# A two-layer trunk: three pairs of gate/up chunks per FFN in seven block products, weight sums by adding DMAs, rows normed before the transposes

## The chip, the cores and the metric

The kernel runs on one core of one Trainium2 chip. The metric is the device time of one execution in microseconds, as the median of the runs. The engines are called as in the profile: PE is the TensorE (PEld its weight loads), DVE the VectorE, ACT the ScalarE, POOL the GpSimd, SP the SyncE, which issues DMAs.

## What is computed

A trunk of two layers on 256 tokens of 1024 numbers, in float32. Each layer is a feed-forward network (FFN) as half a step, a mixer, and a second FFN as half a step; each has a norm ahead and one behind. The FFN's inner width is 2816. The mixer (three kinds of attention, gated and merged) is not changed by the edit beyond names of buffers.

```
def rms_norm(x, gain):
    xf = x.astype(jnp.float32)
    y = xf * lax.rsqrt(jnp.mean(xf * xf, axis=-1, keepdims=True) + NORM_EPS)
    return (y * gain.astype(jnp.float32)).astype(x.dtype)

def swiglu(x, wg, wu, wd):
    return (jax.nn.silu(x @ wg) * (x @ wu)) @ wd
...
    for l in range(DEPTH):
...
        x = x + 0.5 * rms_norm(swiglu(rms_norm(x, g_ffn1_pre[l]), ffn1_wg[l], ffn1_wu[l], ffn1_wd[l]),
                               g_ffn1_post[l])
...
        x = x + rms_norm(mixed, g_mix_post[l])
        x = x + 0.5 * rms_norm(swiglu(rms_norm(x, g_ffn2_pre[l]), ffn2_wg[l], ffn2_wu[l], ffn2_wd[l]),
                               g_ffn2_post[l])
    return x
```

## The kernel before

**Tiles.** The tokens are two tiles of 128, t = 0 and 1. The residual stays in SBUF (`xs`). All weights are streamed from HBM as half-blocks of 128 x 2048 float32 (1 MB each): 33 for an FFN, 40 for a mixer, 212 in all. An FFN is cut in 11 chunks of 256; a chunk's gate and up weights lie side by side, so a gate/up product is 512 columns wide. A gate/up half-block holds four k (blocks of 128 of the 1024 inputs) by 512 columns; a down half-block two k by 1024.

**Float32 by three products.** A weight w is split in whi (a copy by the ScalarE, L88) and wlo = w - whi (VectorE, L89), each in two halves of 1024; the transposed inputs likewise (L198, L199). A product is then hi by hi, hi by lo and lo by hi, three matmuls of 512 columns (`mm3`, L245, L247, L250; L273 in the last down product of a sublayer). One half-block for one token tile is a step of 12 matmuls.

**Order.** Two generators, one for each token tile, go through the trunk; tile 1 is three half-blocks behind tile 0 (`LAG`), and each half-block's split serves both. `Stream` loads ahead through the SyncE's queue into 3 raw buffers and splits into 6 pairs of split buffers. Small chains (transposes of h, attention) run beside the products, a step in each tick. The framework schedules each engine's instructions from the order of the code.

**An FFN** (`ffn`): `prenorm` takes x times the gain (`gained`, L211), transposes it on the TensorE (L197), and makes the reciprocal norm r: Square on the ScalarE (L163), then two steps on POOL (L155, and the power, L157). r enters only behind the products: Silu with scale r (L303), and h = up * r * silu (L305). h is transposed and multiplied by the down weights into an accumulator of two PSUM banks. `postnorm` takes the sums of squares of the accumulator by halves, r by POOL, y (L232), adds it to x (L233), and writes the next sublayer's gained input.

**Names** in rows: f010 is layer 0, second FFN, tile 0; m01 the mixer of layer 0, tile 1; gu the gate/up bank, acc the accumulator, hp a transposed h. PSUM holds two banks for gate/up, four for two accumulators, two for transposes.

Of the kernel before, what the change touches and what calls it, by code (L numbers as in the profile page):

```python
# [8 lines left out]
F32 = mybir.dt.float32  # L9
# [7 lines left out]
P = 128  # L17
# [4 lines left out]
L = 2  # L22
# [15 lines left out]
W_BUFS = 6  # L38
RAW_BUFS = 3
LEAD = 6            # quarter-blocks of weights split ahead of the first lane  # L40
LAG = 3             # half-blocks the second lane of tokens is behind the first
RAMP = 4            # half-blocks in which the lag grows by one at the start
# [3 lines left out]
REST_HEADS, REST_GATE, REST_FFN, REST_FFN_END = 6, 3, 4, 1  # L46
# [8 lines left out]
class Stream:  # L55
    """One half-block of weights after another: loaded, and split into two float32r parts
    whose sum is the float32 weight exactly."""

    def __init__(self, nc, wall, raw, wp):
        self.nc, self.wall, self.raw, self.wp = nc, wall, raw, wp  # L60
        self.raws, self.ready = {}, {}
        self.n = self.loaded = 0

    def load(self, j):
        """Loads run ahead of the splits."""
        while self.loaded < min(j, L * LAYER_BLKS):
# [7 lines left out]
    def split(self, n=1):  # L74
        """The next n quarter-blocks."""
        nc = self.nc
        for _ in range(n):
            i, h = divmod(self.n, 2)
            if i == L * LAYER_BLKS:
                return  # L80
            self.load(i + 1)
            if h == 0:
                self.ready[i] = [self.wp.tile([P, BLK], F32R, tag="w" + c, name=f"w{c}{i}")
                                 for c in ("hi", "lo")]
            c = slice(h * HALF, (h + 1) * HALF)
            hi, lo = (a[:, c] for a in self.ready[i])
            w = self.raws[i][:, c]
            nc.scalar.activation(hi, w, AF.Copy)  # L88
            nc.vector.tensor_sub(lo, w, hi.bitcast(F32))  # L89
            self.n += 1  # L90
            if h:
                self.load(i + 1 + RAW_BUFS)

    def get(self, j):
        self.split(max(0, 2 * (j + 1) - self.n))
        return self.ready[j]
# [3 lines left out]
def trunk(ctx: ExitStack, tc, x, wall, gpre, gpost, lamv, dgain, cst, out):  # L100
# [5 lines left out]
    ps = ctx.enter_context(tc.tile_pool(name="ps", bufs=2, space=PSUM))  # L106

# [9 lines left out]
    # The tensor engine's clock rises under load only: products of zeros until the inputs are here.  # L117
# [50 lines left out]
    def tick():  # L168
        """One step of each chain that began before this half-block."""
# [9 lines left out]
    def start(task):  # L179
        """A chain of small steps beside the products: one step in each half-block."""  # L180
# [24 lines left out]
    xg = {}  # L205
# [7 lines left out]
    def prenorm(t, i, name):  # L213
        """The gained inputs, transposed, and the reciprocals of their norms."""
        src = xg.pop(t)
        r = rstd_of([sumsq(xs[t], D, name)], D, 1, 1.0, name + "r", "rpre")
        xT = pair(KD, name + "T", "xT", NT)
        for a in (0, 4):
            split_T(src, xT, a, 4, f"{name}p{a}")
        yield  # L220
        return xT, r

    def postnorm(t, acc, i, scale, name):
        """Adds the normed product to the residual, by halves."""
        y = sp.tile([P, D], F32, tag="t4", name=name + "y", bufs=4)
        r = rstd_of([sumsq(acc[:, c], D // 2, name + str(n)) for n, c in enumerate(HALVES)],
# [504 lines left out]
```

## Time and profile before

| | us |
|---|---|
| median of the runs (1301.24 to 1301.8) | 1301.6 |
| span of the profiled execution | 1299.8 |
| TensorE busy | 1281.0 |
| VectorE busy | 750.9 |
| ScalarE busy | 707.0 |
| POOL busy | 38.0 |
| an FFN within the trunk, from one last accumulator to the next (451.2 to 640.1) | 188.9 |
| a mixer (189.0 to 451.2) | 262.2 |

The span is the time between the first and the last recorded instruction of one profiled execution, which takes a little less than a run's time. Busy times are sums of instructions on an engine; engines run side by side, so they don't add up to the span. Matmuls are pipelined: a row gives 0.39 us for one, while the next starts 0.23 us after it, so the distance of starts is what one costs.

### The profile page before, as it was taken

The page shows a single profiled execution, that of the slowest core. Times are in us where ns is not written, and L with a number is a line of the kernel's source. Part 1 is how long each engine was busy: PE and PEld are TensorE (multiplying, and loading weights), DVE is VectorE, ACT ScalarE, POOL GpSimd, SP SyncE. Part 2 cuts the span into 40 slices and gives each one's busy share as a digit, 9 for nine tenths or more (in the row PEclk, how much of TensorE's full clock was granted, in tenths as well). Part 3 has the DMA queues.
Part 4 walks back from the last instruction along what each step waited for, and adds up shares of the span by engine and source line. Part 5 has one row for each costly group of instructions (what it writes and reads, how often), then busy time and mean ns, then how long its engine had stood idle before and what let it go on. Part 6 is the DMA issues. An engine that isn't in the chain of part 4 may idle for free.

```text
span 1299.8 us, 15509 instructions
## 1 busy us (share of the span) xinstructions
PE 1281.0 (99%) x6178; PEld 1040.9 (80%) x6178; DVE 750.9 (58%) x973; ACT 707.0 (54%) x1033; POOL 38.0 (3%) x82
## 2 busy tenths in 40 slices
PE   8999999999999999999999999999999999999997
PEld 5888887888877878888788888788888787788885
DVE  6645457656566675445565545666665666644552
ACT  5545446678575554444554444656976655544441
POOL 0000001000000010000000000100000000000000
PEclk9999999999999999999999999999999999999999
DMA  8845555444534555555555555554344444555530
GB/s 310 309 163 194 187 178 202 147 162 136 188 130 171 185 195 194 193 179 183 190 198 191 194 190 179 181 195 162 130 163 164 160 165 174 196 194 185 179 123 32
DMA packets 34056, 232.37 MB, mean 179 GB/s; under 512 B 3904, under 2 KB 4032, under 8 KB 6976
## 3 DMA queue, kind: packets, MB, share of 16 engines
q1 hardware_dynamic: 33264, 230.28, 50.2%
q8 instruction: 48, 0.79, 0.2%
q10 hardware_dynamic: 720, 1.11, 0.2%
q14 instruction: 24, 0.20, 0.0%
HBM read 230.33 MB, written 1.05 MB: 178 GB/s over the span
## 4 chain that ended last, share of the span: by engine, by line
PE 92%; DVE 3%; ACT 2%; issue 1%; POOL 1%; DMA 1%; SPq 0%; POOLq 0%; DVEq 0%; ACTq 0%
PE f000gu L247 2%; PE f000gu L250 2%; PE f000gu L245 2%; PE f001gu L245 1%; PE f011gu L245 1%; PE f101gu L245 1%; PE f111gu L245 1%; PE f111gu L250 1%; PE f101gu L250 1%; PE f011gu L250 1%; PE f001gu L250 1%; PE f011gu L247 1%; PE f001gu L247 1%; PE f101gu L247 1%; PE f111gu L247 1%; PE f010gu L245 1%
## 5 line engine op out<-in xcount | busy, mean ns | idle before, releaser
L89 DVE TENSOR_TENSOR wlo<-raw,whi 128x1024 fp32r<-128x1024 f32 x424 | 506.4, 1222 | 301.2 <-ACT whi L88 300.8
L88 ACT ACTIVATE whi<-raw 128x1024 fp32r<-128x1024 f32 x424 | 432.0, 1055 | 226.0 <-PE f011gu L250 27.0
L245 PE MATMUL f000gu<-whi,f000Th 128*128 128x512 f32 x88 | 35.3, 401 | 0.8 <-ACT f000Th L198 0.8
L245 PE MATMUL f001gu<-whi,f001Th 128*128 128x512 f32 x88 | 35.1, 399 | 0.2 <-ACT f001Th L198 0.2
L245 PE MATMUL f011gu<-whi,f011Th 128*128 128x512 f32 x88 | 35.3, 401 | 0.0
L247 PE MATMUL f000gu<-wlo,f000Th 128*128 128x512 f32 x88 | 35.0, 398 | 0.3 <-DVE wlo L89 0.3
L245 PE MATMUL f111gu<-whi,f111Th 128*128 128x512 f32 x88 | 35.3, 401 | 0.0
L245 PE MATMUL f101gu<-whi,f101Th 128*128 128x512 f32 x88 | 35.2, 400 | 0.0
L250 PE MATMUL f000gu<-whi,f000Tl 128*128 128x512 f32 x88 | 34.9, 397 | 0.0
L245 PE MATMUL f100gu<-whi,f100Th 128*128 128x512 f32 x88 | 34.5, 392 | 0.0
L245 PE MATMUL f010gu<-whi,f010Th 128*128 128x512 f32 x88 | 34.5, 392 | 0.0
L245 PE MATMUL f110gu<-whi,f110Th 128*128 128x512 f32 x88 | 34.4, 391 | 0.0
L250 PE MATMUL f100gu<-whi,f100Tl 128*128 128x512 f32 x88 | 34.4, 391 | 0.0
L250 PE MATMUL f111gu<-whi,f111Tl 128*128 128x512 f32 x88 | 34.4, 391 | 0.0
L250 PE MATMUL f011gu<-whi,f011Tl 128*128 128x512 f32 x88 | 34.4, 391 | 0.0
L250 PE MATMUL f101gu<-whi,f101Tl 128*128 128x512 f32 x88 | 34.4, 391 | 0.0
L250 PE MATMUL f001gu<-whi,f001Tl 128*128 128x512 f32 x88 | 34.4, 390 | 0.0
L247 PE MATMUL f010gu<-wlo,f010Th 128*128 128x512 f32 x88 | 34.3, 390 | 0.0
L247 PE MATMUL f110gu<-wlo,f110Th 128*128 128x512 f32 x88 | 34.3, 390 | 0.0
L247 PE MATMUL f100gu<-wlo,f100Th 128*128 128x512 f32 x88 | 34.3, 390 | 0.0
L247 PE MATMUL f011gu<-wlo,f011Th 128*128 128x512 f32 x88 | 34.3, 389 | 0.0
L250 PE MATMUL f110gu<-whi,f110Tl 128*128 128x512 f32 x88 | 34.3, 389 | 0.0
(1889 smaller groups left out, 3154.6 us busy)
## 6 DMA issues: line engine op xcount, KB each, us to landing
raw<-wall_dram SPq DMA_DIRECT2D x211, 1024.0 KB, 4.8
gpre<-gpre_dram SPq DMA_DIRECT2D x6, 512.0 KB, 6.2
gpost<-gpost_dram SPq DMA_DIRECT2D x6, 512.0 KB, 4.0
raw<-wall_dram SPq DMA_DIRECT2D x2, 512.0 KB, 7.9
out_dram<-x ACTq DMA_DIRECT2D x4, 256.0 KB, 2.0
x<-x_dram SPq DMA_DIRECT2D x2, 256.0 KB, 3.0
x<-x_dram SPq DMA_DIRECT2D x1, 512.0 KB, 9.1
cs<-cst_dram SPq DMA_DIRECT2D x1, 352.0 KB, 11.5
```

The costliest lines, as they stand in the source:

```text
L88: nc.scalar.activation(hi, w, AF.Copy)
L89: nc.vector.tensor_sub(lo, w, hi.bitcast(F32))
L245: nc.tensor.matmul(o[:, n:n + 512], xh[:, k, :], wh[:, kk, n:n + 512], start=first, stop=False)
L247: nc.tensor.matmul(o[:, n:n + 512], xh[:, k, :], wl[:, kk, n:n + 512], start=False, stop=False)
L250: nc.tensor.matmul(o[:, n:n + 512], xl[:, k, :], wh[:, kk, n:n + 512], start=False, stop=last)
```

## The change

**Seven block products.** In each FFN the chunks (1,2), (4,5) and (7,8) are taken as pairs. Two token tiles by two halves of k, times two halves of k by two chunks, is a product of 2 x 2 blocks; instead of eight block products it is made of seven, p1 to p7. The left sides are blocks of the transposed inputs or their row sums S1 to S4 (`sums`, VectorE L408 and L411, ScalarE L410; the transposes are also kept unsplit for them, L276). The right sides are B11, B21, B22 and the sums T1 = B11 + B12, T2 = T1 + B22, T3 = B12 + B22 and T4 = T2 + B21 of the stored half-blocks, each made in place in a raw buffer. Each of the seven is split like a half-block and used for one step. So a pair is split seven times where it was four. T2 and T4 are added by the VectorE (L134, two of 128 x 1024 each); T1 and T3 by a DMA that POOL issues and that adds HBM's block onto the raw buffer (L118): T1's when B11 is split, T3's right behind the load of B12. Products collect in three PSUM banks X, Y and Z; results are combined by one copy (L465) and five VectorE steps of 128 x 512 for each pair. The other chunks (0, 3, 6, 9, 10) stay plain products.

**Rows normed first.** FFN inputs are x * r * gain (`normed`, L296) before they are transposed, so Silu and h take no r. The mixers keep the old way.

**Order and buffers.** `program()` writes out a list of steps; weights come in the order of use. W_BUFS is 5 and RAW_BUFS 5; the two transposing banks became `tr` and `z`, the latter shared with Z. Norm steps, splits of transposes and combinations are scheduled early (`soon`). In the last eight blocks of a mixer tile 1 is four half-blocks behind.

```diff
-W_BUFS = 6
-RAW_BUFS = 3
...
+W_BUFS = 5
+RAW_BUFS = 5
...
+DMA_SUMS = ("T1", "T3")
...
+    def recipe(self, k):
+        if isinstance(k, int):
+            return [("split", k, c, (k,) if c else (), 2) for c in range(2)]
+        name, (b11, b12, b21, b22) = k
+        at, plus, free = {"B11": (b11, None, ()), "T1": (b11, b12, ()), "B21": (b21, None, ()),
+                          "T2": (b11, b22, ()), "B22": (b22, None, ()),
+                          "T3": (b12, b22, (b12, b22)), "T4": (b11, b21, (b11, b21))}[name]
+        ops = [("add", at, plus, c) for c in range(2)] if plus is not None and name not in DMA_SUMS else []
+        ops += [("split", at, c, free if c else (), 2) for c in range(2)]
+        after = {"B11": ("T1", b11, b12), "T1": ("T2", b11, b22), "T2": ("T4", b11, b21)}.get(name)
+        if after and after[0] in DMA_SUMS:
+            ops += [("dma", *after[1:])]
+        return ops
...
+        while self.loaded < len(self.blocks) and len(self.raws) < most:
+            i = self.blocks[self.loaded]
...
+            if i in self.thirds:
+                self.add_by_dma(i, self.thirds[i])
+    def add_by_dma(self, at, plus):
+        self.nc.gpsimd.dma_start(self.raws[at], self.wall[plus], accum_op=ALU.add)
...
+        if op[0] == "dma":
+            self.add_by_dma(*op[1:])
+        elif op[0] == "add":
+            c = slice(op[3] * HALF, (op[3] + 1) * HALF)
+            nc.vector.tensor_add(self.raws[op[1]][:, c], self.raws[op[1]][:, c], self.raws[op[2]][:, c])
...
+    tr_tags = itertools.cycle(("tr", "z"))
+    def tr_tile(shape, name, tag=None):
+        return ps.tile(shape, F32, tag=tag or next(tr_tags), name=name, bufs=1)
...
+    def normed(t, i):
+        with soon():
+            r = rstd_of([sumsq(xs[t], D, f"n{i}{t}")], D, 1, 1.0, f"n{i}{t}r", "rpre")
+            xg[t] = sp.tile([P, D], F32, tag="t4", name=f"xg{i}{t}", bufs=4)
+            for c in HALVES:
+                nc.vector.scalar_tensor_tensor(xg[t][:, c], xs[t][:, c], r, gain("pre", i)[:, c],
+                                               op0=ALU.mult, op1=ALU.mult)
...
-            nc.vector.scalar_tensor_tensor(y[:, c], acc[:, c], r, g[:, c], op0=ALU.mult, op1=ALU.mult)
-            nc.vector.tensor_add(xs[t][:, c], xs[t][:, c], y[:, c])
-            if i + 1 < 3 * L:
-                gained(t, i + 1, c)
-            else:
-                nc.scalar.dma_start(out[t * P:(t + 1) * P, c], xs[t][:, c])
+            with soon():
+                nc.vector.scalar_tensor_tensor(y[:, c], acc[:, c], r, g[:, c],
+                                               op0=ALU.mult, op1=ALU.mult)
+                nc.vector.tensor_add(xs[t][:, c], xs[t][:, c], y[:, c])
+                if i + 1 == 3 * L:
+                    nc.scalar.dma_start(out[t * P:(t + 1) * P, c], xs[t][:, c])
+                elif (i + 1) % 3 == 1:
+                    gained(t, i + 1, c)
+        if i + 1 < 3 * L and (i + 1) % 3 != 1:
+            normed(t, i + 1)
...
+        def sums(self):
+            (a11, a12), (a21, a22) = ([quads[t][:, k:k + 4] for k in (0, 4)] for t in range(2))
+            self.S = {}
+            for n, o, x, op, y in (("1", a22, a21, ALU.subtract, a22), ("2", a22, a22, ALU.subtract, a11),
+                                   ("3", a11, a11, ALU.subtract, a21), ("4", a12, a12, ALU.add, a22)):
+                nc.vector.tensor_tensor(o, x, y, op=op)
+                hi, lo = self.S[n] = pair(4, f"{self.nm}S{n}", "k2", 8)
+                nc.scalar.activation(hi, o, AF.Copy)
+                nc.vector.tensor_sub(lo, o, hi.bitcast(F32))
+            quads.clear()
...
+            if n in "14":
+                t = 0 if n == "1" else 1
+                return [b[:, 4 * t:4 * t + 4] for b in self.xT[t]]
+            if n == "2":
+                return [b[:, 4:] for b in self.xT[0]]
+            return self.S[{"5": "1", "6": "2", "7": "3", "3": "4"}[n]]
...
+        def up(self, t, c, hb, k):
...
+                self.o[t] = ps.tile([P, 512], F32, tag="gu", name=f"{self.nm}{t}gu{c}")
+            for _ in block(self.o[t], [b[:, 4 * hb:4 * hb + 4] for b in self.xT[t]], k, hb == 0, hb == 1):
...
+        def seven(self, n, c, k):
...
+            bank = {"1": "X", "2": "X", "5": "Z", "3": "Z"}.get(n, "Y")
...
+            if n in "156":
+                tag = "z" if bank == "Z" else "gu"
+                o[bank] = ps.tile([P, 512], F32, tag=tag, name=nm + bank, bufs=1 if bank == "Z" else 2)
+            for _ in block(o[bank], self.left(n), k, n in "156", True):
+                pass
+            o = o[bank]
...
+            q = self.c
+            with soon():
+                if n == "1":
+                    q["s1"] = tmp("s1", "mg")
+                    nc.scalar.activation(q["s1"], o, AF.Copy)
+                elif n == "5":
+                    q["s15"] = tmp("s15", "mg")
+                    nc.vector.tensor_sub(q["s15"], o, q["s1"])
+                elif n == "2":
+                    self.act(0, c, o, tmp("h11", "tok"))
+                elif n == "6":
+                    q["u2"] = tmp("u2", "mg")
+                    nc.vector.tensor_add(q["u2"], o, q["s1"])
+                elif n == "3":
+                    nc.vector.tensor_sub(q["u2"], o, q["u2"])
+                    self.act(0, c + 1, q["u2"], q["u2"])
+                elif n == "7":
+                    nc.vector.tensor_sub(q["s15"], q["s15"], o)
+                    self.act(1, c + 1, q["s15"], q["s15"])
+                elif n == "4":
+                    nc.vector.tensor_add(q["s1"], q["s1"], o)
+                    self.act(1, c, q["s1"], q["s1"])
...
+    for i in range(MIX_BLKS):
+        lag = LAG if i < MIX_BLKS - 8 else LAG + 1
+        order += [(i + lag - 0.5, 1, j + i), (i, 0, j + i)]
...
+    def seven(c, e, rest, last=()):
+        r = iter(rest)
+        def more():
+            return [x for x in [next(r, None)] if x]
+        out = [p(c, "1"), u(0, e, 0), u(0, e, 1), p(c, "5"), p(c, "2")] + more()
+        out += [u(1, e, 0), u(1, e, 1), p(c, "6")] + more() + [p(c, "3")] + more()
+        return out + [p(c, "7")] + more() + [*last[:1], p(c, "4"), *last[1:]]
```

In the order of the program the change is to be seen at three places. First, POOL at the end of layer 0's mixer, where the second FFN begins. m00or and m01or are the reciprocals for the mixer's results, f010r the one of the next FFN's inputs. Before:

```order
L155 TENSOR_SCALAR m00or<-m00o0s 128x1 [waits Activation_49]
L155 TENSOR_SCALAR m00or<-m00o1s,m00or 128x1 [waits Activation_49,Pool_49]
L157 TENSOR_TENSOR m00or<-m00or,nhalf 128x1 [waits Pool_49]
L155 TENSOR_SCALAR f010r<-f010s 128x1 [waits Activation_49]
L157 TENSOR_TENSOR f010r<-f010r,nhalf 128x1 [waits Pool_49]
L155 TENSOR_SCALAR m01or<-m01o0s 128x1 [waits Activation_49]
L155 TENSOR_SCALAR m01or<-m01o1s,m01or 128x1 [waits Activation_49,Pool_49]
L157 TENSOR_TENSOR m01or<-m01or,nhalf 128x1 [waits Pool_49]
```

After; n20r and n21r are the FFN's reciprocals (the FFN is called f2 now), and raw is a raw weight buffer:

```order
L221 TENSOR_SCALAR m00or<-m00o0s 128x1 [waits Activation_49]
L221 TENSOR_SCALAR m00or<-m00o1s,m00or 128x1 [waits Activation_49,Pool_49]
L223 TENSOR_TENSOR m00or<-m00or,nhalf 128x1 [waits Pool_49]
L118 DMA raw_3636<-wall_dram 128x2048 [waits DMAHW3_49,DMAHW4_49,DMAHW2_49,DMAHW5_49,DMAHW1_49,DMAHW6_49,DMAHW0_49,DMAHW7_49,DMASW4_49,DVE_49]
L221 TENSOR_SCALAR n20r<-n20s 128x1 [waits Activation_49]
L223 TENSOR_TENSOR n20r<-n20r,nhalf 128x1 [waits Pool_49]
L118 DMA raw_3490<-wall_dram 128x2048 [waits DMAHW0_49,DVE_49]
L221 TENSOR_SCALAR m01or<-m01o0s 128x1 [waits Activation_49]
L221 TENSOR_SCALAR m01or<-m01o1s,m01or 128x1 [waits Activation_49,Pool_49]
L223 TENSOR_TENSOR m01or<-m01or,nhalf 128x1 [waits Pool_49]
L221 TENSOR_SCALAR n21r<-n21s 128x1 [waits Activation_49]
L223 TENSOR_TENSOR n21r<-n21r,nhalf 128x1 [waits Pool_49]
```

Two DMAs now stand among the small steps: the one for a T3 ahead of n20r, the one for a T1 ahead of m01or; each waits for loads or splits.

Second, the VectorE at the same place, from the scaling of the mixer's result to the first split transposes. Before:

```order
L232 SCALAR_TENSOR_TENSOR m00oy<-m00acc,m00or,gpost_3628 128x512 [waits Activation_49,Pool_49]
L232 SCALAR_TENSOR_TENSOR m00oy<-m00acc,m00or,gpost_3628 128x512
L233 TENSOR_TENSOR x_73<-x_73,m00oy 128x512 [waits DVE_49] x2
L211 TENSOR_TENSOR xg_3632<-x_73,gpre_3633 128x512 [waits DVE_49]
L89 TENSOR_TENSOR wlo_3649<-raw_3526,whi_3648 128x1024 [waits DMAHW1_49,Activation_49]
L211 TENSOR_TENSOR xg_3632<-x_73,gpre_3633 128x512 [waits DVE_49]
L89 TENSOR_TENSOR wlo_3649<-raw_3526,whi_3648 128x1024 [waits Activation_49]
L199 TENSOR_TENSOR f010Tl<-f010p_3675,f010Th 128x512 [waits Activation_49]
L89 TENSOR_TENSOR wlo_3721<-raw_3563,whi_3720 128x1024 [waits DMAHW2_49]
```

After:

```order
L323 SCALAR_TENSOR_TENSOR m00oy<-m00acc,m00or,gpost_3626 128x512 [waits Activation_49,Pool_49]
L323 SCALAR_TENSOR_TENSOR m00oy<-m00acc,m00or,gpost_3626 128x512
L325 TENSOR_TENSOR x_73<-x_73,m00oy 128x512 [waits DVE_49]
L274 TENSOR_TENSOR m01gT1l<-m01gp_3646,m01gT1h 128x512 [waits Activation_49]
L325 TENSOR_TENSOR x_73<-x_73,m00oy 128x512 [waits DVE_49]
L144 TENSOR_TENSOR wlo_3660<-raw_3434,whi_3659 128x1024 [waits DMAHW7_49,Activation_49]
L144 TENSOR_TENSOR wlo_3660<-raw_3434,whi_3659 128x1024 [waits Activation_49]
L144 TENSOR_TENSOR wlo_3693<-raw_3490,whi_3692 128x1024 [waits DMAHW0_49,Activation_49]
L144 TENSOR_TENSOR wlo_3693<-raw_3490,whi_3692 128x1024 [waits Activation_49]
L296 SCALAR_TENSOR_TENSOR xg_3687<-x_73,n20r,gpre_3688 128x512 [waits DVE_49,Pool_49]
L296 SCALAR_TENSOR_TENSOR xg_3687<-x_73,n20r,gpre_3688 128x512 [waits DVE_49]
L144 TENSOR_TENSOR wlo_3723<-raw_3538,whi_3722 128x1024 [waits DMAHW1_49,Activation_49]
L274 TENSOR_TENSOR f20Tl<-f20p_3714,f20Th 128x512 [waits Activation_49]
```

The multiplication that makes xg no longer follows the addition to x; four splits (L144) stand between, and it waits for POOL.

Third, the VectorE between two pairs of the second FFN. Before, splits, products h (L305) and split transposes (L199):

```order
L89 TENSOR_TENSOR wlo_4115<-raw_4000,whi_4114 128x1024 [waits DMAHW5_49,Activation_49]
L199 TENSOR_TENSOR f011hT2l<-f011hp_4109,f011hT2h 128x256 [waits Activation_49]
L89 TENSOR_TENSOR wlo_4115<-raw_4000,whi_4114 128x1024 [waits Activation_49]
L199 TENSOR_TENSOR f010hT3l<-f010hp_4134,f010hT3h 128x256 [waits Activation_49]
L89 TENSOR_TENSOR wlo_4153<-raw_4038,whi_4152 128x1024 [waits DMAHW6_49,Activation_49]
L89 TENSOR_TENSOR wlo_4153<-raw_4038,whi_4152 128x1024 [waits Activation_49]
L305 SCALAR_TENSOR_TENSOR f011h_4187<-f011gu_4139,f011r,f011s_4185 128x256 [waits DVE_49,Activation_49]
L89 TENSOR_TENSOR wlo_4192<-raw_4077,whi_4191 128x1024 [waits DMAHW7_49,Activation_49]
```

After, from B11's split of the pair (7,8) (wlo_4505) to T1's (wlo_4585, from the same raw buffer):

```order
L144 TENSOR_TENSOR wlo_4505<-raw_4413,whi_4504 128x1024 [waits DMAHW3_49,Activation_49]
L426 TENSOR_TENSOR f2c4u_4405<-f2c4u_4405 128x256 [waits Activation_49]
L144 TENSOR_TENSOR wlo_4505<-raw_4413,whi_4504 128x1024
L478 TENSOR_TENSOR f2c4s_4301<-f2c4s_4301,f2c4Y 128x512 [waits PE_49]
L144 TENSOR_TENSOR wlo_4524<-raw_4415,whi_4523 128x1024 [waits DMAHW4_49,Activation_49]
L426 TENSOR_TENSOR f2c4s_4301<-f2c4s_4301 128x256 [waits Activation_49]
L274 TENSOR_TENSOR f20hT_4457<-f20hp_4495,f20hT_4457 128x256 [waits Activation_49]
L144 TENSOR_TENSOR wlo_4549<-raw_4440,whi_4548 128x1024 [waits DMAHW5_49,Activation_49]
L274 TENSOR_TENSOR f21hT_4503<-f21hp_4543,f21hT_4503 128x256 [waits Activation_49]
L481 TENSOR_TENSOR f2c4s_4249<-f2c4s_4249,f2c4Y 128x512 [waits PE_49]
L144 TENSOR_TENSOR wlo_4585<-raw_4413,whi_4584 128x1024 [waits DMASW2_49,Activation_49]
L426 TENSOR_TENSOR f2c4s_4249<-f2c4s_4249 128x256 [waits Activation_49]
```

Combinations (L478, L481) stand among the splits, and T1's split waits for the adding DMA (DMASW) as well as for the ScalarE.

## Rows read from the trace of the kernel before

**Rows 1.** Page, busy us of each engine (share of the span), instructions.
```profile
PE 1281.0 (99%) x6178; PEld 1040.9 (80%) x6178; DVE 750.9 (58%) x973; ACT 707.0 (54%) x1033; POOL 38.0 (3%) x82
```

**Rows 2.** Page, the chain that ended last, share of the span by engine.
```profile
PE 92%; DVE 3%; ACT 2%; issue 1%; POOL 1%; DMA 1%; SPq 0%; POOLq 0%; DVEq 0%; ACTq 0%
```

**Rows 3.** Windows: stretch, length, busy us (instructions), granted clock, DMA share, GB/s.
```profile
207.00:455.00 248.00, 247.57 (x1317) 200.81 (x1316) 153.56 (x216) 161.86 (x246) 4.57 (x9) 1.00 0.46 164
...
470.00:643.00 173.00, 172.17 (x782) 141.52 (x782) 90.83 (x109) 79.10 (x108) 1.11 (x2) 1.00 0.54 189
...
1283.00:1300.00 17.00, 8.01 (x36) 5.99 (x34) 6.04 (x10) 2.80 (x9) 2.00 (x6) 0.86 0.16 62
```

**Rows 4.** Waits of the TensorE: us in total, times, longest us.
```profile
PE f000p L197 <- DVE xg L211: 2.1, 1, 2.1
...
PE f111p L197 <- DVE xg L211: 0.8, 1, 0.8
```

**Rows 5.** Timeline, TensorE, twelve matmuls: start us, us, line, operation.
```profile
186.29 0.39 PE L245 MATMUL f001gu<-whi,f001Th 128*128 128x512 f32 x1
...
189.01 0.39 PE L273 MATMUL f000acc<-whi,f000hT10h 128*128 128x512 f32 x1
```

**Rows 6.** Page, the costliest groups: out<-in xcount | busy, mean ns | idle before.
```profile
L89 DVE TENSOR_TENSOR wlo<-raw,whi 128x1024 fp32r<-128x1024 f32 x424 | 506.4, 1222 | 301.2 <-ACT whi L88 300.8
L88 ACT ACTIVATE whi<-raw 128x1024 fp32r<-128x1024 f32 x424 | 432.0, 1055 | 226.0 <-PE f011gu L250 27.0
```

**Rows 7.** Timeline within an FFN, VectorE: two splits back to back; a split transpose.
```profile
64.83 0.42 DVE L199 TENSOR_TENSOR f001hT2l<-f001hp,f001hT2h 128x256 fp32r<-128x256 f32 x1
...
78.19 2.36 DVE L89 TENSOR_TENSOR wlo<-raw,whi 128x1024 fp32r<-128x1024 f32 x2 [0.47 <-ACT whi L88]
```

**Rows 8.** VectorE's instructions by line and shape: busy us, mean ns.
```profile
L305 DVE SCALAR_TENSOR_TENSOR f101h<-f101gu,f101r,f101s 128x256 f32<-128x256 f32 x11 | 5.3, 484 | 23.8 <-ACT f101s L303 23.8
...
L232 DVE SCALAR_TENSOR_TENSOR m01oy<-m01acc,m01or,gpost 128x512 f32<-128x512 f32 x2 | 1.5, 750 | 1.1 <-POOL m01or L157 1.1
...
L548 DVE TENSOR_TENSOR m01bs<-m01bs,m01by 128x512 f32<-128x512 f32 x2 | 1.4, 689 | 2.5 <-PE m01by L250 2.5
```

**Rows 9.** Page, DMA: a queue's packets, MB, share; an issue's count, KB, us to landing.
```profile
q1 hardware_dynamic: 33264, 230.28, 50.2%
...
raw<-wall_dram SPq DMA_DIRECT2D x211, 1024.0 KB, 4.8
```

**Rows 10.** Timeline where layer 0's mixer ends and its second FFN begins.
```profile
453.57 0.39 PE L273 MATMUL m00acc<-whi,m00gT1l 128*128 128x512 f32 x1
...
454.00 0.60 ACT L163 ACTIVATE m00o0j<-m00acc 128x512 f32<-128x512 f32 x1 [0.73 <-PE m00acc L273]
...
455.79 0.55 POOL L157 TENSOR_TENSOR m00or<-m00or,nhalf 128x1 f32<-128x1 f32 x1
...
456.37 1.41 DVE L232 SCALAR_TENSOR_TENSOR m00oy<-m00acc,m00or,gpost 128x512 f32<-128x512 f32 x2 [1.66 <-POOL m00or L157]
...
457.70 1.28 DVE L233 TENSOR_TENSOR x<-x,m00oy 128x512 f32<-128x512 f32 x2
...
459.08 1.06 ACT L163 ACTIVATE f010j<-x 128x1024 f32<-128x1024 f32 x1 [0.35 <-DVE x L233]
```

**Rows 11.** Timeline of the start, a power on POOL beside VectorE work.
```profile
13.02 1.28 DVE L211 TENSOR_TENSOR xg<-x,gpre 128x512 f32<-128x512 f32 x2
...
14.22 1.22 DVE L89 TENSOR_TENSOR wlo<-raw,whi 128x1024 fp32r<-128x1024 f32 x1
14.44 1.41 POOL L157 TENSOR_TENSOR f001r<-f001r,nhalf 128x1 f32<-128x1 f32 x1
```

**Rows 12.** Timeline of the start, tile 0's norm and its gained input.
```profile
5.87 0.54 POOL L157 TENSOR_TENSOR f000r<-f000r,nhalf 128x1 f32<-128x1 f32 x1
...
8.40 1.29 DVE L211 TENSOR_TENSOR xg<-x,gpre 128x512 f32<-128x512 f32 x2 [7.29 <-DMA gpre<-gpre_dram]
```

More of the change, by code (lines that the diff above doesn't have):

```diff
@@ new lines, in room, with step @@
+    def room(self, k):
+        i = self.items.index(k, max(0, len(self.ready) - 1))
+        return i < W_BUFS or self.last[self.items[i - W_BUFS]] < self.now
+    def step(self):
+        nc = self.nc
+        k, op = self.ops[self.done]
+        self.load()
+        if op[0] == "dma":
[3 more added lines that the diff above has]
+            nc.vector.tensor_add(self.raws[op[1]][:, c], self.raws[op[1]][:, c], self.raws[op[2]][:, c])
+        else:
+            _, at, n, free, of = op
+            if k not in self.ready:
+                self.ready[k] = [self.wp.tile([P, BLK], F32R, tag="w" + c, name=f"w{c}{len(self.ready)}")
@@ L94, in get, with ahead @@
-    def get(self, j):
-        self.split(max(0, 2 * (j + 1) - self.n))
-        return self.ready[j]
+            for f in free:
+                del self.raws[f]
+        self.done += 1
+        self.load()
+    def ahead(self, most):
+        while self.done < len(self.ops) and most > 0:
+            k = self.ops[self.done][0]
+            if self.first[k] > self.now + AHEAD or not self.room(k):
+                return
+            self.step()
+            most -= 1
+    def get(self, k):
+        while k not in self.ready or (self.done < len(self.ops) and self.ops[self.done][0] == k):
+            self.step()
+        return self.ready[k]
@@ L524, in mixer @@
         nm = f"m{l}{t}"
-        xT, r = yield from prenorm(t, 3 * l + 1, nm)
+        pre = prenorm(t, 3 * l + 1, nm)
+        xT, r = next(pre)
+        next(pre)
+        yield
+        next(pre)
+        yield
         rq = sp.tile([P, 2], F32, tag="rq", name=nm + "rq", bufs=2)
@@ L576, in mixer @@
             n = f"{nm}{mx}"
[L577 removed]
+            y = ys[mx] = pair(4, n + "y", "mT", 8)
             if mx == "a":
@@ L644, in trunk, with run @@
-    go(1, False)
+    now = {}
+    gains_of = {}
+    def run(step, k):
+        kind, n, t, *a = step
+        l, sub = divmod(n, 3)
+        if k is not None:
+            waiting[:] = side
+            w.ahead(4)
+        else:
+            waiting[:] = []
+        if n not in now:
+            j = l * LAYER_BLKS + (0, FFN_BLKS, FFN_BLKS + MIX_BLKS)[sub]
+            now[n] = [mixer(t, l, j) for t in range(NT)] if sub == 1 else FFN(n, j)
+        if sub == 1:
+            next(now[n][t], None)
+        else:
+            getattr(now[n], kind)(t, *a, *((k,) if k is not None else ()))
+        if k is not None:
+            w.now += 1
@@ new lines, in trunk, with program @@
+    with tc.manual_schedule(engines={nc.scalar.engine, nc.vector.engine}):
+        normed(0, 0)
+        for _ in range(2):
+            w.step()
+        for n, (step, k) in enumerate(plan[:START]):
+            run(step, k)
+            if n == 1:
+                normed(1, 0)
+    for n, (step, k) in enumerate(plan[START:]):
+        if n == CONSTANTS:
+            constants()
+        run(step, k)
+def program():
+    out = []
+    for n in range(3 * L):
+        l, sub = divmod(n, 3)
+        j = l * LAYER_BLKS + (0, FFN_BLKS, FFN_BLKS + MIX_BLKS)[sub]
+        steps = mixer_steps(n, j) if sub == 1 else ffn_steps(n, j)
+        if n:
+            i = max(i for i, (_, k) in enumerate(out) if k is not None)
+            out.insert(i + 1, steps.pop(1))
+            out.insert(i, steps.pop(0))
+        out += steps
+    return out
```

292 lines of the change are left out of this document (161 added, 131 removed).

## The prediction

> **What bounds the kernel now.** Read first how busy each engine is: the TensorE is busy in 99% of the span, the VectorE in 58% [rows 1]. Then the chain that ended last: 92% of it lies on the TensorE [rows 2]. Then the waits: the largest that the TensorE shows is 2.1 us at the start, the next of its kind 0.8 [rows 4]; all that the view lists come to some 10 us. The windows say the same stage by stage: 172.2 of 173 us in a feed-forward network (FFN), 247.6 of 248 in a mixer; the granted clock is 1.00 there, the upper level, 2.4 GHz [rows 3]. So time can only be won by fewer products, and lost where the TensorE begins to wait. A product of 512 columns starts every 0.2267 us: twelve from 186.29 to 189.01 [rows 5].
>
> The profiled execution has a span of 1299.8 us; the median of the runs is 1301.6, so 1.8 us lie around the span. I sum against 1299.8 and add 1.8.
>
> **A. Fewer products.** By the planned order the kernel issues 5088 products of 512 columns before and 4944 after. This is seven block products where there were eight, three products of each of four k: 12 fewer for each of 12 pairs of chunks, 144 in all. The transposes stay as many. 144 x 0.2267 = **-32.6 us**. All of it lies on the path as long as nothing else comes to bind; it is also the most that the change can win.
>
> **B. Rows normed before they are transposed.** Before, the transposes needed only x times its gain, and the reciprocal norm came in later, at the Silu. Now they need Square of x, two POOL steps and a multiplication first. This counts at three places, where an FFN follows another sublayer (mixer to FFN twice, FFN to FFN once). The chain, from the rows of the first mixer's end [rows 10]: last product of token tile 0 at 453.57, over at 454.0; squares and POOL until 456.34 (2.4 us); two scalings and two additions until 459.0 (2.7); Square of x and its accumulator 1.25; POOL's two steps between 0.7 and 1.4; the first half of the multiplication 0.7. That makes 8.4 to 8.8 us. Over it lie, by the order of after, 44 products and four transposes of tile 1, about 10.4 us, so the bare chain is covered. But on the VectorE the order of after has four weight splits between the additions and the multiplication, 4 x 1.14 = 4.6 us [rows 7], of which the Square and POOL hide some 2.2. With them tile 0's first half is ready at about 11 us, 0.5 late. For tile 1 the cover is 36 products and four transposes, 8.7 us, against a chain of 8.4 plus one transposed split and a weight split that share the VectorE: 0.5 to 2 us late. Then the four row sums S1 to S4 (eight VectorE steps of 0.69 [rows 8]) crowd the next splits. I take +3 us for each place, **+9 us** (0, all covered, to +18, twice as much).
>
> Two things sit on POOL there. Its small steps run longer beside VectorE instructions that read two tensors from SBUF: the power took 0.55 us at 455.79 and 1.41 beside the splits near 14.44 [rows 10, 11]. The Trainium skill states this as a rule (SBUF — State Buffer, section "Who interferes with whom"): a VectorE instruction with two SBUF inputs contends with a GpSimd instruction that reads SBUF; by it each of 2 x 3 norms would come about 0.9 us later, +5 us, and the total some 1288; the two rows agree with it in sign. And POOL now issues the adding DMAs in order: in the order of after, tile 0's pre-norm stands behind the DMA that makes a T3, which waits until that block's load has landed.
>
> **C. A VectorE that is busier in the pairs.** A steady pair of 17 half-block steps costs the TensorE 204 x 0.2267 = 46.2 us and some 1.6 for transposes, 48 us. In it the VectorE has 12 blocks of two splits at 1.14 (27.4) [rows 7], four additions of 1024 (4.6, like a split), five combinations of block products at 0.69 (3.4), six products h at 0.48 (2.9) and six split transposes at 0.42 (2.5) [rows 7, 8]: 40.8 of 48 us, 85%, where it was 90.8 of 173 [rows 3]. It still fits, but bunching leaves less room: a split may come late behind a combination. Three places are tight: p2 must wait until p1's result is copied out of the bank that both use (about 0.6 us, hidden in steady pairs by the steps between, not in the first pair), T2 must be added and split between T1's and its own use, and five weight buffers stand where six stood. I take 0.4 us for each pair, **+5 us** (0 to +10; a gain is excluded, since the TensorE waits for nothing there before). The ScalarE adds 72 copies of 1024 elements (76 us at 1055 ns [rows 6]) and smaller ones, to about 62%: no bound.
>
> Over the whole span the VectorE goes from 751 to about 961 us: 72 splits and 48 additions at 1.22, 92 steps of 512 at 0.69.
>
> **D. The adding DMAs.** T1 = B11 + B12 can start only when B11 is split, and must be there before p5. In the order of after that leaves the transfer 9 to 11.6 us until T1's own split could begin, and the TensorE stalls only past some 13. No row shows such a DMA. The nearest is the plain load of 1 MB, 4.8 us from issue to landing, on queues whose packets take half of the engines' time [rows 9]. One that reads two operands is bounded below by 4.8 and, taken as two plain reads, comes to 9.6; four times the plain load, 19.2, is my upper bound. I take 9.6, nearest to the row: **0 us**. T3 has more than a step's time to spare. In a sentence apart: the Trainium skill (DMA: Bandwidth & Descriptors, section "Measured (HBM→SBUF, 128 partitions, SWDGE, issued from GpSimd)") gives 6.15 us for a plain megabyte issued from GpSimd, which no run here shows; with twice that, 12.3 us, an estimate, the sum would stay as it is.
>
> **E. The rest.** Start: POOL ends the reciprocal norm at 6.4 us, before the gain is there at 8.4 [rows 12], so norming first costs nothing there. Mixers: five weight buffers for six leave four steps of lead where there were six, and two in the last eight blocks (lag 4); a step is 2.7 us and a split 2.3, so 0 to +3 in all; I take 0. The end (8.0 us of products in the last 17 us [rows 3]) is not touched.
>
> **Sum.** 1299.8 - 32.6 + 9 + 5 + 0 = 1281.2 us of span, and 1.8 around it: **1283 us**.
>
> **Rivals.**
> 1. All covered: B and C cost 0 to 6 together, since the chain of 8.4 us is under its cover of 10.4. 1269 to 1276 us. For it: the TensorE waits nearly nowhere now. Against: four splits in front of the multiplication.
> 2. Losses a little larger than summed (B at its upper end or C at 10): 1292 to 1299.
> 3. POOL's queue holds the norms: a T3 DMA waits for a load that was issued late, and the norm behind it comes 5 us later, 3 x 5 = 15: 1298. It decides when the load lands later than 6.4 us after tile 0's last product.
> 4. The VectorE becomes the bound in the pairs: at full durations (1.22 for 1.14) the 40.8 us of a pair are 43.0, and if waits in between add a sixth, the pair takes 50.2 for 48: +2.2 x 12 = 26, 1309, slower. It decides where waits and work on the VectorE pass 48 us in a pair, and the whole gain is gone at 49.6. For it: 85% of busy time with many short dependences; against: half of it can be done early.
> 5. The adding DMAs are late: at 19.2 us each T1 stalls p5 by about 6 us, 12 x 6 = 72: about 1355, slower. The place is the wait of T1's split for its DMA, on ScalarE and VectorE, with all later splits queued behind it. It breaks even where a pair's net gain, 18.6 / 12 = 1.6 us, is used up: at about 14.6 us for a DMA. For it: no row shows an adding DMA's speed. Against: 9.6 is well below.
> 6. The change doesn't do what it says, and the TensorE's products come slower (a cadence of 0.233 would undo the whole gain: 4944 x 0.0063 = 31 us). Against: left and right operands have the same form. It is within the slower cases' chance.
>
> **How the numbers follow.** Forecast (1276 to 1292) 0.50; all covered 0.17; larger losses 0.10; POOL's queue 0.06; the VectorE 0.06; DMAs late 0.10; other 0.01. The range reaches from 1269 to 1301, which holds the first four, 0.83, less a little at the edges. A difference of 0.2% (2.6 us, 1299.0 to 1304.2) is about what a measurement of this kernel can tell from no change. Faster takes the first three and two thirds of the fourth, 0.81; the same 0.04; slower 0.15.
>
> **What would show it.** Right: 4944 products at the same 0.2267; an FFN within the trunk about 7 us shorter (8.2 less for products, 1.2 more for its pairs); the VectorE at 75%; the waits of the TensorE at f2, f3 and f5's first transposes 1 to 3 us each; the adding DMAs landing within 11 us. Wrong: p5 waiting for T1's split in every pair (rival 5); waits for weight splits all over the pairs (rival 4); POOL idle before a pre-norm because of a DMA (rival 3); waits inside the mixers (E).

## The result, and the profile after

The changed kernel takes 1312.9 us (1309.6 to 1314.2 in four runs) where the kernel before takes 1301.65: a ratio of 1.0087, interval 1.0072 to 1.0101. The forecast was 1283 us, with a range of 1269 to 1301. It is slower, not faster, and 30 us away from the forecast.

The page of the profiled execution (span 1310.9 us), busy time of each engine and the chain that ended last:

```profile
PE 1260.9 (96%) x6034; PEld 1018.4 (78%) x6034; DVE 931.4 (71%) x1185; ACT 787.4 (60%) x1149; POOL 72.1 (6%) x106
...
PE 34%; DMA 6%; DVE 4%; ACT 2%; POOL 1%; issue 1%; POOLq 0%; DVEq 0%; ACTq 0%; SPq 0%
DMA raw<-wall_dram 6%; DVE wlo L144 2%; ACT whi L143 1%; PE f51gu L344 1%; PE f51gu L339 1%; PE f51gu L341 1%; PE f50acc L339 1%; PE f50acc L341 1%; PE f50acc L344 1%; DVE raw L134 1%; PE f51acc L344 0%; PE f51acc L341 0%; PE f51acc L339 0%; PE m11b L339 0%; PE m11a L339 0%
```

Against [rows 1] the TensorE has 144 instructions less, as planned, but stands still for 50 us of the span where it was 19. In the chain, DMA into the raw weight buffers now holds 6%, against 1% in all in [rows 2]. The waits of the TensorE say where (us in total, times, longest):

```profile
PE f5c4Z L339 <- ACT whi L143: 6.5, 1, 6.5
PE f2c4Z L339 <- ACT whi L143: 3.6, 1, 3.6
PE f3c4Z L339 <- ACT whi L143: 3.4, 1, 3.4
PE f31hp L271 <- DVE f3c4s L426: 2.4, 1, 2.4
PE f00gu L339 <- DVE f0c4s L481: 2.4, 1, 2.4
```

f2c4Z is p5 of the pair (4,5) in the FFN f2: it waits for the split of T1. What [rows 9] was for plain loads, with the queue of POOL's DMAs (q0) new, on the page (a queue's packets, MB, share of 16 engines; then an issue's count, KB, median us to landing):

```profile
q1 hardware_dynamic: 33264, 230.28, 47.4%
q0 software_dynamic: 3456, 25.17, 10.0%
...
raw<-wall_dram SPq DMA_DIRECT2D x211, 1024.0 KB, 4.9
raw<-wall_dram POOLq DMA_DIRECT2D x24, 1024.0 KB, 11.4
```

An adding DMA lands after 8.1 to 18.0 us, 11.4 in the median. The stages, from the last product into tile 0's accumulator to the next (before; after; and two kernels of the experiments, all sums on the VectorE, and p5 moved):

| us | before | after | all sums on VectorE | p5 two steps later |
|---|---|---|---|---|
| to the end of the first FFN | 191.5 | 194.9 | 183.9 | 185.4 |
| first mixer | 262.1 | 261.1 | 261.1 | 261.1 |
| second FFN | 188.9 | 190.0 | 183.1 | 182.5 |
| third FFN | 188.6 | 190.3 | 181.9 | 181.3 |
| second mixer | 262.1 | 261.5 | 261.1 | 261.2 |
| fourth FFN | 188.8 | 193.5 | 182.8 | 183.8 |
| rest | 17.9 | 19.6 | 19.6 | 19.9 |

Each FFN should have become 8.2 us shorter (36 products of 0.2267), less what the new steps cost; instead each became 1.1 to 4.7 longer. The mixers are as they were.

One such wait in the timeline of after (start, us, engine, line, operation, and the idle time before):

```profile
520.50 1.83 POOL L118 DMA_DIRECT2D raw<-wall_dram  x2 [41.59 <-DVE wlo L144]
...
524.65 0.42 ACT L425 ACTIVATE f2c1s<-f2c1s 128x256 f32<-128x256 f32 x1 [0.23 <-DVE f2c1s L481]
...
534.82 0.39 PE L344 MATMUL f20gu<-whi,f20Tl 128*128 128x512 f32 x1
537.70 2.00 ACT L143 ACTIVATE whi<-raw 128x1024 fp32r<-128x1024 f32 x2 [12.63 <-DMA raw<-wall_dram]
538.78 2.36 DVE L144 TENSOR_TENSOR wlo<-raw,whi 128x1024 fp32r<-128x1024 f32 x2 [12.37 <-ACT whi L143]
...
538.80 0.79 PE L339 MATMUL f2c4Z<-whi,f2S1h 128*128 128x512 f32 x1 [3.60 <-ACT whi L143]
...
541.08 0.63 PE L339 MATMUL f2c4Z<-whi,f2S1h 128*128 128x512 f32 x1
...
541.51 0.63 PE L341 MATMUL f2c4Z<-wlo,f2S1h 128*128 128x512 f32 x1
```

At 520.50, when B11 is split, POOL issues two adding DMAs of the pair (4,5) together, T3's and behind it T1's. The first lands 8.6 us after its issue, the second, T1's, 16.4. (T3's goes first in six of the twelve pairs, the three (4,5) among them; in the first FFN and in the pairs (7,8) T1's does.) ScalarE stands for 12.6 us before T1's copy, with all that is queued behind it, and VectorE with it; the TensorE runs dry for 3.6 us. Then its products start 0.43 us apart (541.08, 541.51) instead of 0.227, at the lower of its two clock levels (1.2 GHz); the granted clock of the windows falls with it (stretch, length, busy us (instructions), granted clock, DMA share, GB/s):

```profile
520.00:540.00 20.00, 16.00 (x71) 12.40 (x69) 7.63 (x11) 4.57 (x8) 1.83 (x2) 0.94 0.91 253
540.00:560.00 20.00, 19.94 (x81) 16.25 (x82) 20.00 (x24) 14.03 (x20) 0.00 (x0) 0.89 0.36 129
```

Here this costs 2.0 us on top (ten starts, from 540.06 to 544.38, take 4.3 us instead of 2.3).

### The profile page after: what moved, and what is told of

Read it like the earlier page. It is cut to its first block, busy times and chain, and to the rows that moved or that the text cites. A ratio compares the mean times of both kernels' runs of the same rounds, so it can differ in the third digit from the quotient of the medians.

```text
span 1310.9 us, 15665 instructions
## 1 busy us (share of the span) xinstructions
PE 1260.9 (96%) x6034; PEld 1018.4 (78%) x6034; DVE 931.4 (71%) x1185; ACT 787.4 (60%) x1149; POOL 72.1 (6%) x106
## 3 DMA queue, kind: packets, MB, share of 16 engines
q1 hardware_dynamic: 33264, 230.28, 47.4%
q0 software_dynamic: 3456, 25.17, 10.0%
HBM read 255.49 MB, written 1.05 MB: 196 GB/s over the span
## 5 line engine op out<-in xcount | busy, mean ns | idle before, releaser
L144 DVE TENSOR_TENSOR wlo<-raw,whi 128x1024 fp32r<-128x1024 f32 x496 | 589.4, 1220 | 174.7 <-ACT whi L143 174.2
L143 ACT ACTIVATE whi<-raw 128x1024 fp32r<-128x1024 f32 x496 | 503.5, 1055 | 242.8 <-DMA raw<-wall_dram 94.3
L134 DVE TENSOR_TENSOR raw<-raw,raw 128x1024 f32<-128x1024 f32 x48 | 57.8, 1218 | 0.0
L118 POOL DMA_DIRECT2D raw<-wall_dram x24 | 21.7, 942 | 467.8 <-DMA raw<-wall_dram 216.7
L339 PE MATMUL f00gu<-whi,f00Th 128*128 128x512 f32 x40 | 17.4, 435 | 4.3 <-DVE f0c4s L481 2.4
L721 ACT ACT_TABLE_LOAD x12 | 15.4, 1283 | 6.4 <-PE m01bg L344 2.2
L341 PE MATMUL f00gu<-wlo,f00Th 128*128 128x512 f32 x40 | 16.7, 417 | 0.4 <-DVE wlo L144 0.4
L344 PE MATMUL f00gu<-whi,f00Tl 128*128 128x512 f32 x40 | 16.8, 419 | 0.2 <-DVE f00Tl L274 0.2
L339 PE MATMUL f30gu<-whi,f30Th 128*128 128x512 f32 x40 | 16.2, 404 | 0.1
L339 PE MATMUL f20gu<-whi,f20Th 128*128 128x512 f32 x40 | 16.2, 406 | 0.0
L339 PE MATMUL f50gu<-whi,f50Th 128*128 128x512 f32 x40 | 16.2, 405 | 0.0
## 6 DMA issues: line engine op xcount, KB each, us to landing
raw<-wall_dram POOLq DMA_DIRECT2D x24, 1024.0 KB, 11.4
```

Source lines behind the costliest of these rows:

```text
L118: self.nc.gpsimd.dma_start(self.raws[at], self.wall[plus], accum_op=ALU.add)
L134: nc.vector.tensor_add(self.raws[op[1]][:, c], self.raws[op[1]][:, c], self.raws[op[2]][:, c])
L339: nc.tensor.matmul(o[:, n:n + 512], xh[:, k, :], wh[:, kk, n:n + 512], start=first, stop=False, **kw)
L341: nc.tensor.matmul(o[:, n:n + 512], xh[:, k, :], wl[:, kk, n:n + 512], start=False, stop=False, **kw)
L344: nc.tensor.matmul(o[:, n:n + 512], xl[:, k, :], wh[:, kk, n:n + 512], start=False, stop=last, **kw)
L721: nc.scalar.activation(s, o, AF.Sigmoid, scale=r)
```

## Experiments

Theory A: what costs is an adding DMA that stands in front of a split which the in-order engines then wait for; T1's is late because another goes ahead of it or runs beside it, and because its split comes early in the order. Theory B: the VectorE is the bound in the pairs. Theory C: the bytes moved cost, by slower loads, wherever the DMAs stand. In the first expectations theory A is narrower: there T1's DMA is late only because it is second in its queue; runs 3 and 5 made it wider. Times are medians; all ratios are to the kernel before, run on the same chip (1299.7 to 1300.4 us).

**1. T3's DMA behind T1's split, in the code.**

```diff
             ops += [("dma", *after[1:])]
+        if name == "T1" and "T3" in DMA_SUMS:
+            ops += [("dma", b12, b22)]
...
-            if i in self.thirds:
-                self.add_by_dma(i, self.thirds[i])
```

> The one edit: T3's adding DMA is issued behind T1's split instead of right behind the load of its block, so T1's adding DMA no longer stands second. Theory A (T1's transfer is late because T3's goes ahead of it: 8 to 10 us alone, 14 to 18 as the second of two): the three waits of p5 in the pair (4,5), 3.4 to 6.5 us, go, and with them the slow products behind them; the FFNs lose about 6 to 10 us each, the time comes to 1285 to 1292. Theory B (the VectorE is the bound in the pairs, and T1's transfer only starts late because B11's split is late): at most 3 us less, 1309 to 1313. Theory C (adding DMAs and loads share engines, whichever goes first): about half, near 1300.

1312.67 us, 1.0113 (1.0065 to 1.0161; one of the four runs took 1325.1). It tells nothing of the theories: the scheduler put POOL's instructions in the same order as before, since T3's DMA depends on nothing that T1's split makes.

**2. No adding DMA, T1 and T3 split as they are.**

```diff
-        self.nc.gpsimd.dma_start(self.raws[at], self.wall[plus], accum_op=ALU.add)
+        pass
```

> No adding DMA at all: T1 and T3 are split as they stand, without the addition, so part of the computation is left out; all other instructions stay. This gives what the transfers cost in all. Theory A and C: 1280 to 1288, no wait of p5 for a split, loads back at about 5 us. Theory B: within 4 us of the changed kernel, 1309 to 1313, with the waits of h's transposes for the VectorE still there.

1275.81 us, 0.9808 (0.9791 to 0.9825): all that the adding DMAs cost is 37 us, more than any theory said. Theory B is out as the main cause.

**3. T1 alone by DMA**, T3 by the VectorE: `DMA_SUMS = ("T1",)`.

> T3 is added by the VectorE (24 more additions of 1024, 29 us in all), T1 still by DMA, alone in POOL's queue. Theory A: T1 lands within 8 to 11 us, p5's waits go, and 2.4 us more VectorE work for a pair costs 0 to 1 us each: 1285 to 1300. Theory B: slower than the changed kernel, 1315 to 1340.

1294.57 us, 0.9945 (0.9926 to 0.9964). T1's DMAs land in 8.1 to 11.3 us, and yet they cost 18.5 us against the run that follows. The timeline at the same pair shows how:

```profile
511.57 0.94 POOL L118 DMA_DIRECT2D raw<-wall_dram  x1 [40.23 <-DMA raw<-wall_dram]
...
516.93 0.69 DVE L481 TENSOR_TENSOR f2c1s<-f2c1s,f2c1Y 128x512 f32<-128x512 f32 x1
...
521.96 2.00 ACT L143 ACTIVATE whi<-raw 128x1024 fp32r<-128x1024 f32 x2 [5.10 <-DMA raw<-wall_dram]
...
523.87 0.40 ACT L425 ACTIVATE f2c1s<-f2c1s 128x256 f32<-128x256 f32 x1
...
524.88 0.66 PE L271 MATMUL f21hp<-ident,f2c1s 128*128 128x128 f32 x2 [2.94 <-DVE f2c1s L426]
...
526.62 0.63 PE L339 MATMUL f20gu<-whi,f20Th 128*128 128x512 f32 x1
...
527.05 0.63 PE L341 MATMUL f20gu<-wlo,f20Th 128*128 128x512 f32 x1
```

The Silu of the last pair's result (L425) had its input at 517.6, when L481 was done. It stands behind T1's copy on the ScalarE, which waits 5.1 us for the DMA; so the transposes of that h wait 2.9 us, and the products behind them start 0.43 us apart again. p5 itself does not wait in this FFN. What the TensorE wants first is not T1, but what stands behind T1 in a queue.

**4. All sums on the VectorE:** `DMA_SUMS = ()`.

> All four sums on the VectorE (48 more additions, 58 us). Theory A: no transfers to wait for; the VectorE's 40.8 us in a pair of 48 become 45.6, so it is close to the bound: 1290 to 1310. Theory B: 4.9 us more in each of 12 pairs, 1350 to 1370.

1276.04 us, 0.9811 (0.9794 to 0.9827): 58 us more of additions on the VectorE than in the changed kernel (53 more of its busy time), and 37 us less time. No expectation held. The page:

```profile
PE 1250.0 (98%) x6034; PEld 1015.2 (80%) x6034; DVE 984.6 (77%) x1233; ACT 788.6 (62%) x1149; POOL 52.1 (4%) x82
```

The VectorE has room even at 77%; against run 2, which leaves those additions out, they cost nothing that can be measured.

**5. T1's DMA really ahead of T3's:** as 1, with both kept in the order of the code on POOL.

> Both adding DMAs stay, but T1's now really goes ahead of T3's in POOL's queue (in the run before the scheduler had put T3's first again); T3's is issued right behind it. Theory A (what costs is that T1's transfer is second in its queue): T1 lands in 8 to 11 us and the time comes to that of the kernel with T1's DMA alone, 1291 to 1298. Theory C (each adding DMA costs by what it takes from the loads and from the other, in whichever order): 1307 to 1314, T1 landing in 11 us or more.

1305.25 us, 1.0034 (1.0014 to 1.0053), between the theories. The order in the queue is worth some 7 us (by the two ratios, 0.0053 of 1300). T3's DMA, right behind, still runs beside T1's. T1's lands sooner now, after 7.7 to 12.4 us; what comes late is the plain load behind it. The pair (4,5) again:

```profile
522.73 1.76 POOL L118 DMA_DIRECT2D raw<-wall_dram  x2 [42.10 <-DVE wlo L144]
...
531.31 2.01 ACT L143 ACTIVATE whi<-raw 128x1024 fp32r<-128x1024 f32 x2 [3.88 <-DMA raw<-wall_dram]
...
538.62 2.01 ACT L143 ACTIVATE whi<-raw 128x1024 fp32r<-128x1024 f32 x2 [5.30 <-DMA raw<-wall_dram]
```

The ScalarE waits 3.9 us for T1's DMA and then 5.3 us for a plain load, which took 13.5 us beside the two adding DMAs instead of 4.9.

**6. T3's DMA only after T1's split:** as 5, with a VectorE step ahead of T3's DMA, in program order behind T1's split.

```diff
+            ops += [("late", b12, b22)]
...
+        elif op[0] == "late":
+            nc.vector.tensor_sub(self.raws[op[1]][:, :1], self.raws[op[1]][:, :1], self.zero1)
             self.add_by_dma(*op[1:])
```

> As the run before, and T3's DMA also waits until T1 is split (a VectorE step of one column ahead of it), so that the two adding DMAs never run at the same time. Theory A: as T1's DMA alone, 1291 to 1298, T1 8 to 9 us. Theory C: 1300 to 1312, since the same bytes are moved, with loads beside T3's DMA still at 8 us or more.

1295.63 us, 0.9963 (0.9942 to 0.9984): as T1's DMA alone (run 3), with the same bytes moved as in the changed kernel. The edit does only part of what it is meant to: the VectorE step depends on nothing that T1's split makes, and in five of the twelve pairs it ran before T1's DMA had landed, so that the two still overlap there:

```profile
562.43 0.15 DVE L133 TENSOR_TENSOR raw<-raw,zero 128x1 f32<-128x1 f32 x1
...
562.99 0.88 POOL L118 DMA_DIRECT2D raw<-wall_dram  x1 [0.76 <-DVE raw L133]
...
572.46 1.06 ACT L146 ACTIVATE whi<-raw 128x1024 fp32r<-128x1024 f32 x1 [4.33 <-DMA raw<-wall_dram]
```

What the ScalarE's copies waited for in these runs, in us (times):

| | changed kernel | 3, T1 alone | 5, T1 first | 6, T3 later | 4, none |
|---|---|---|---|---|---|
| adding DMAs | 57.5 (9) | 34.8 (8) | 21.6 (5) | 38.1 (8) | 0 |
| plain loads | 36.8 (19) | 10.6 (7) | 47.0 (18) | 26.5 (16) | 6.8 (7) |

From run 5 to run 6 the waits for adding DMAs grow and those for plain loads shrink by 20 us, and the time falls by 10. So there is some truth in theory C, but not wherever the DMAs stand: the loads are late where two adding DMAs run together. That T3's transfer costs little by itself is shown by runs 9 and 11.

**7. Only T3 by DMA:** `DMA_SUMS = ("T3",)`.

> Only T3 by DMA; T1 is added by the VectorE (1276.0 with none by DMA, 1294.6 with T1 alone). T3 is needed some 16 us later than T1. Theory A: nothing waits for it, 1275 to 1282. Theory C: as dear as T1's, 1291 to 1298, with loads beside it at 8 us and waits of the ScalarE for them.

1298.51 us, 0.9969 (0.9942 to 0.9995). It does not test what it should. T3 is made in the buffer that T1's addition reads, so T1 now adds a T3, and waits for its DMA; the adding DMA is on T1's path again (T1's additions, L134, wait 30.9 us for it in eight places), and costs 22 us, with runs from 1287 to 1313 us.

**8. No block products,** row sums left away, all chunks plain in the old order of the two tiles.

> No block products: all chunks as eight plain products, the row sums left away, rows still normed before the transposes, the two tiles in the old order with five weight and five raw buffers. This prices the norm in front of the transposes alone, against the kernel before: by the prediction's term B +3 us at each of three places, 1305 to 1312; if the norm is covered but for what the kernel with all sums on the VectorE shows at these places (about 1 us each), 1301 to 1305.

1314.52 us, 1.0110 (1.0093 to 1.0127): 14 us slower than before, more than either figure. Waits of the TensorE around the second and third FFN:

```profile
PE f31p L271 <- DVE xg L296: 1.7, 1, 1.7
PE f30p L271 <- DVE xg L296: 1.5, 1, 1.5
PE f21acc L377 <- ACT f21hT L273: 1.3, 1, 1.3
PE f20gu L344 <- DVE f20Tl L274: 1.2, 1, 1.2
```

The waits for the normed rows (f20, f30, f31) are 1 to 2 us each. The wait of f21acc is of my own order's making: it lacks the shorter rest that the kernel before gives the last h (`REST_FFN_END`). The three FFNs behind another sublayer take 193.7 to 194.5 us, 5 to 6 more than before. How the 14 us divide between the norm and the order stays open.

**9. T3 alone by DMA, off T1's path:** as 7, with T3's DMA issued behind T1's additions.

> T1 by the VectorE; T3 by DMA, issued when T1's additions have read its block, so no other adding DMA runs and T3 is needed some 11 us later or more. (In the run with T3 alone before this one, T3 was made before T1 had read its block, so T1 had to wait for that DMA.) Theory A, what costs is an adding DMA in front of a split that the in-order engines then wait for: 1275 to 1281. Theory C, the bytes moved cost, by slower loads: 1284 to 1298.

1279.01 us, 0.9840 (0.9823 to 0.9858): 3.0 us above run 4. As theory A has it.

**10. T1 alone by DMA, p5 two steps later.**

```diff
-        out = [p(c, "1"), u(0, e, 0), u(0, e, 1), p(c, "5"), p(c, "2")] + more()
-        out += [u(1, e, 0), u(1, e, 1), p(c, "6")] + more() + [p(c, "3")] + more()
+        out = [p(c, "1"), u(0, e, 0), u(0, e, 1), p(c, "2")] + more()
+        out += [p(c, "5"), u(1, e, 0), u(1, e, 1), p(c, "6")] + more() + [p(c, "3")] + more()
```

> T1 by DMA, T3 by the VectorE (1294.6 in the old order), and in the pairs (4,5) and (7,8) and in the first FFN's pairs p5 stands two steps later, behind p2 and a down step; T1's split stands as much later in the queues of ScalarE and VectorE. Theory A: 5.4 us more for a transfer of 8 to 11 us hides it, 1276 to 1284. Theory C: 1290 to 1297 as before.

1278.66 us, 0.9837 (0.9821 to 0.9853): 15.9 us less than run 3. Of the 18.5 us of T1's DMA all but 2 or 3 were the place of its split.

**11. The changed kernel with p5 two steps later,** both DMAs as they are.

> The changed kernel with p5 two steps later. Theory A: T1, second in the queue, lands 14 to 18 us after its issue, which two steps do not hide wholly: 1285 to 1302. Theory C: 1306 to 1313.

1275.34 us, 0.9814 (0.9798 to 0.9829): 37.6 us faster than the changed kernel (35 to 36 by the two ratios), more than theory A said. The reason is on POOL, in the timeline at the pair (4,5):

```profile
510.29 0.93 POOL L118 DMA_DIRECT2D raw<-wall_dram  x1 [41.38 <-DVE wlo L144]
521.32 0.86 POOL L118 DMA_DIRECT2D raw<-wall_dram  x1 [10.10 <-ACT whi L143]
```

With p5 later, the loads of its blocks come later too, and so T3's DMA: the two are now 11 us apart instead of together. The page, and the windows from 480 to 620 us of this kernel and of the changed one:

```profile
raw<-wall_dram POOLq DMA_DIRECT2D x24, 1024.0 KB, 8.7
...
480.00:620.00 140.00, 140.00 (x635) 114.88 (x634) 118.44 (x140) 84.36 (x114) 3.54 (x4) 1.00 0.75 248
```

```profile
480.00:620.00 140.00, 135.93 (x605) 110.36 (x605) 117.43 (x139) 83.48 (x115) 3.60 (x4) 0.98 0.68 233
```

DMAs land in 8.7 us instead of 11.4, and the TensorE is busy throughout, with 30 products more in the same 140 us.

**12. The control: all sums on the VectorE, p5 later.**

> All sums on the VectorE with p5 two steps later: the control for the two runs before. Without an adding DMA the order of steps should matter little: 1274 to 1280 by both theories, 1276.0 in the old order.

1276.28 us, 0.9818 (0.9800 to 0.9836): the order of steps alone is worth nothing (1276.04 in run 4).

So the 37 us are, as an estimate: T1's split too early for its DMA, 18 to 20 (run 3 or 6 against 4); T3's DMA beside T1's, through plain loads that come late, some 10 (run 5 against 6, and perhaps more, as the two still overlap in five pairs of run 6); and T3's ahead of T1's, some 7 (the changed kernel against 5). Each of the last two is uncertain by 2 to 4 us, as runs 5 and 6 scatter by 9 to 10 us. Runs 4, 11 and 12 beat both kernels alike, by 23 to 24 us against before.

## Why the prediction was wrong

**A, fewer products: right.** In run 4 the TensorE is busy for 1250.0 us against 1281.0: 31.0 less, for 32.6 summed. In the changed kernel itself it is 20.1, since products run slower behind the long waits.

**D, the adding DMAs: the step that failed.** It put them at 0 us, and they cost 37. The duration was not the error: 9.6 us were taken, and a DMA that runs alone or first mostly takes 8 to 10.5. Three readings were wrong. First, the step took T1's DMA by itself, while the order of after showed T3's ahead of it on POOL; it was weighed for the norms only (rival 3), not for T1. As the second of two, T1's took 14.3, 15.3 and 16.4 us in the three pairs (4,5) where p5 waits, about rival 5's break-even of 14.6. Second, "the TensorE stalls only past some 13" asked when p5 needs T1, not who stands behind T1's split. On the ScalarE the next Silu does, and run 3 shows a loss with a DMA of 10.3 us. Third, the step did not ask what two adding DMAs do to the plain loads beside them: in run 5, where T1's DMA goes first, the ScalarE waits 47.0 us for plain loads and 21.6 for adding DMAs; in run 4, without them, 6.8 for plain loads. Rival 5 named this queue, and was the right case; its size (72 us at 19.2) was too large, as no adding DMA of the changed kernel took longer than 18.0 us and only the pair (4,5) had p5 itself waiting, in three of the four FFNs.

**B and C, +14: too dear.** Run 4 has them both, with more VectorE work than summed, and its span of 1273.5 is 6.3 above the 1267.2 that products alone would give. The waits of the TensorE for normed rows at an FFN's start add up to 2.0 to 2.4 us at each of the three places, where before had 0.3 to 1.3: some 4 us more in all, not 9. So the bare chain was nearly covered, as its sum said (the terms give 8.2 to 8.9 us from the start of the last product, not 8.4 to 8.8, which changes nothing). This holds for the order of the change; in run 8, in another order, each of these FFNs is 5 to 6 us longer than before. Rival 4 (the VectorE becomes the bound) is out with runs 2 and 4. By the Trainium skill's rule that a VectorE instruction with two SBUF inputs contends with a GpSimd instruction that reads SBUF (SBUF — State Buffer, section "Who interferes with whom"), the prediction would have added 5 us. The trace of run 4 agrees in sign: the first POOL step of each of the six norms took 0.96 to 1.05 us, where it took 0.19 at the start. But with all waits at these places grown by some 4 us, the 5 us are not all there.

**E, the rest: small errors.** The mixers lost nothing (261.1 for 262.1). The first product of the changed kernel starts 1.4 us later, at 12.6 us (it waits 1.9 us for its transposed inputs, 0.8 in before), and the end is 1.8 us longer, since tile 1's last product now stands 10.9 us behind tile 0's, where it stood 9.2.

## What to carry to other kernels

Where a transfer feeds an in-order engine, ask what stands behind the waiting instruction in that engine's queue, and not only when its own result is needed. Count the transfers that become ready together: the one on the critical path may be second, and the plain loads beside them may come late. When the engine that would do the work has slack at 77%, let it; or move the consumer a few steps in the order, which here was worth some 36 us in two lines.

## What the runs showed of the hardware

An adding DMA of 1 MB lands after 7.9 to 10.9 us when no other adding DMA runs (run 9, median 8.2), against a median of 4.9 for a plain load; by the page its packets take 0.61 us (10.0% of 16 x 1310.9 us over 3456) where a plain load's take 0.30 (47.4% over 33264), at about the same size. Plain loads issued beside a pair of them land after 11 to 15 us. And a wait of 2.9 us of the TensorE was followed by some 13 products 0.43 us apart (run 3, from 525.77), so that the wait cost nearly twice its length.
